# Output projections by token tile, x tiles normed one at a time, a larger ring, and loads issued by ScalarE

## The chip, the cores and the metric

One Trainium2 chip; the kernel is one launch on one NeuronCore. The metric is the device time of the launch in microseconds (us). The core's engines each run their own instruction stream in order: TensorE (PE: matmuls and transposes), VectorE (DVE), ScalarE (ACT), GpSimd (POOL) and SyncE (SP, which here only issues loads). They wait for each other, and for transfers, by semaphores.

## The reference, cut to what matters

Everything is fp32. `first_block` runs two layers on x (256 tokens of width 1024) and, in layer 0 only, on a context of 256 tokens:

```
mod = silu(c) @ w_mod[i] + b_mod[i]                  # six vectors: shifts, scales and gates
h   = modulate(rmsnorm(x) * g_pre_mix, shift, scale)
y   = concat(MLA attention, short conv, two-way SSD)(h @ w_in) @ w_out
x   = x + gate * rmsnorm(y) * g_post_mix
h   = modulate(rmsnorm(x) * g_pre_ffn, shift2, scale2)
x   = x + gate2 * rmsnorm(relu(h @ w_ff1)**2 @ w_ff2) * g_post_ffn
```

`second_block` then runs two attention mixers, a (dilated windows) and b (sliding window with sinks). After each:

```
x = layer_norm(ALPHA * x + attn(x @ w_in) @ w_out, ln_g, ln_b)
x = x + sigmoid(x @ ple_w_gate) * (p @ ple_w_proj)
```

## The kernel before

**Tiles.** Tokens come in tiles of 128: tiles 0 and 1 are the context (`CTX`), tiles 2 and 3 are x (`X`; t2 and t3 below). A residual tile is two halves of 128x512. Products with a weight block are built from 128x512 or 128x256 matmuls over 8 slices of the inner dimension (`KT`).

**fp32 from three matmuls.** Each operand is split in a high part (ACT cast, line 226) and a low part (DVE or POOL subtract, line 227); `mm3` (line 207) runs three matmuls per slice: high x high, high x low, low x high. Weights come through SP in `raw` tiles of 512 KB (`wblk`, line 170, issue at line 180; five such tiles). Their two parts go to the pools `wh` and `wl` of ten tiles each, or, for the last `keep` slices, into the `un` ring, where they may stay. Rings `qn`, `pn` and `rn` hold other working tiles.

**Norms.** `postnorm` (line 427) takes the sum of squares of a projected tile (ACT, line 431), multiplies by the gate (POOL and DVE, line 432), forms the root on POOL (lines 167 and 168) and adds to the residual (DVE, line 435). `normed` (line 400) does the same kind of chain for the next norm: ACT line 406, POOL 167 and 168, DVE 410. `modulated` (line 414) transposes a normed tile on PE (line 420), applies scale and shift while it evicts (DVE, line 424) and splits the result (lines 226, 227).

**The places of the change.** `out_projection(i)` (line 877) multiplies the mixer's output by `w_out`, column block 0 for all tiles and then column block 1, and calls `postnorm` and `done` as tiles are complete: in layer 0 for the pair X, then for the pair CTX; in layer 1 for t2 and then t3. `done` (`mid0`, line 1297; `mid1`, line 1319) is norm and modulation for the FFN, whose first block in layer 0 (lines 935 and 937) computes the columns of X, then those of CTX. `second(i)` (line 1227) is `w_out` of a mixer, the deep norm and the gate: block 0 for both tiles, block 1 for both tiles, then layer norm (DVE lines 1241 to 1250) and transposes (line 998); its rows of `ln_g` and `ln_b` are broadcast by SP (`brow`, line 235). `load_cols(1)` (line 247) loads 8 small vectors of layer 1 (line 254), transposes them (line 257) and copies them (line 259). `load_mask` (line 1028) and the rope tables (lines 1326, 1328) are small loads issued by POOL.

**What sets the order.** Each engine's order is fixed at build: a scheduler with a modelled timeline goes through the program (line 1362) and takes instructions by readiness and by the priority that decorators give some functions. Loads of all engines share a few completion semaphores; an issue that reuses one waits first until the transfer that used it before has landed.

## Time and profile before

| | |
|---|---|
| runs | 1542.83, 1542.24, 1540.04 us; median 1542.24 us |
| profiled execution | 1545.77 us; span of its trace 1544.0 us; mean granted PE clock 0.984 |
| PE busy | 1474.4 us, 95% of the span, 8417 matmuls and transposes |
| DVE, ACT, POOL busy | 67%, 48%, 20% of the span |
| DMA | 235.46 MB, 153 GB/s on average |

Busy shares are of the span. A matmul row shows a start and a modelled duration; matmuls are pipelined, so the distance from one start to the next is the pace. "idle before" is what an engine waited just before the row, and the arrow names what released it.

### The profile page before, as it was taken

What the parts mean: (1) busy time and instruction counts of PE and PEld (TensorE: products, weight loads), DVE (VectorE), ACT (ScalarE), POOL (GpSimd) and SP (SyncE); (2) the same over time, 40 slices, a digit from 0 to 9 for tenths busy, and PEclk for the clock granted to TensorE, in tenths of its full rate; (3) what the DMA queues carried; (4) which work ended last, traced back from release to release, by engine and by line L of the source; (5) the groups of instructions that cost most, each with busy time, mean ns of one, the idle gap of its engine ahead of it and who ended that gap; (6) DMA issues with size and microseconds to landing.
All of it is one profiled execution on the core that took longest, in us unless ns stands there. A gap on an engine that the chain in (4) does not pass through costs nothing.

```text
span 1544.0 us, 23412 instructions
## 1 busy us (share of the span) xinstructions
PE 1474.4 (95%) x8417; PEld 1216.4 (79%) x8417; DVE 1036.5 (67%) x2053; ACT 740.0 (48%) x1590; POOL 307.3 (20%) x356
## 2 busy tenths in 40 slices
PE   5997999999999999998999899999999999999998
PEld 3666678888878888877897688997888889878886
DVE  3559556378597557477886756676775786476866
ACT  3433335463233333245556655564566457445663
POOL 1225201151011110034330301112310320021110
PEclk9998999999999999999999999999999999999999
DMA  8844722226366546323423546555436550645442
GB/s 285 272 165 134 254 82 83 89 61 213 110 210 210 179 141 209 124 81 110 124 74 111 174 137 206 191 193 174 152 108 199 162 182 13 216 147 167 140 148 69
DMA packets 129575, 235.46 MB, mean 153 GB/s; under 512 B 11536, under 2 KB 29139, under 8 KB 129459
## 3 DMA queue, kind: packets, MB, share of 16 engines
q1 hardware_dynamic: 128576, 232.42, 47.0%
q0 software_dynamic: 704, 1.50, 0.3%
q8 instruction: 66, 1.08, 0.3%
q14 instruction: 50, 0.41, 0.1%
q10 hardware_dynamic: 179, 0.06, 0.0%
HBM read 232.82 MB, written 1.11 MB: 152 GB/s over the span
## 4 chain that ended last, share of the span: by engine, by line
PE 81%; DVE 9%; DMA 5%; issue 2%; ACT 2%; POOL 1%; SPq 0%; ACTq 0%; DVEq 0%; POOLq 0%
PE sc L212 46%; PE mm L212 19%; PE tp L459 3%; DVE wl L227 2%; PE fl L303 2%; DMA raw<-in_w_mod_dram 2%; DMA raw<-in_ple_w_gate_dram 1%; DVE u L778 1%; PE mm L635 1%; PE sc L1079 1%; PE fl L212 1%; PE sc L789 1%; PE sc L630 1%; DMA raw<-in_w_in_dram 1%; PE sc L1104 1%
## 5 line engine op out<-in xcount | busy, mean ns | idle before, releaser
L227 DVE TENSOR_TENSOR wl<-raw,wh 128x512 fp32r<-128x512 f32 (+1 forms) x602 | 418.8, 731 | 143.5 <-ACT wh L226 140.3
L226 ACT CAST wh<-raw 128x512 fp32r<-128x512 f32 (+1 forms) x602 | 357.5, 622 | 304.0 <-PE sc L212 112.2
L212 PE MATMUL sc<-wh,u 128*128 128x512 f32 (+2 forms) x1416 | 459.0, 392 | 2.3 <-DVE u L962 1.0
L212 PEld LDWEIGHTS sc<-wh,u 128*128 128x128 f32 x1416 | 265.5, 190 | 57.6 <-DVE u L962 2.2
L212 PE MATMUL sc<-wl,u 128*128 128x512 f32 (+2 forms) x708 | 274.1, 389 | 0.2
L212 PE MATMUL sc<-u,wh 128*128 128x256 f32 (+1 forms) x1072 | 264.2, 336 | 2.6 <-ACT wh L226 1.8
L212 PE MATMUL mm<-wh,u 128*128 128x512 f32 (+1 forms) x648 | 218.6, 393 | 1.6 <-ACT u L226 1.2
L212 PEld LDWEIGHTS sc<-u,wh 128*128 128x128 f32 x1072 | 183.8, 191 | 25.3 <-ACT wh L226 2.7
L212 PE MATMUL sc<-u,wl 128*128 128x256 f32 (+1 forms) x536 | 178.0, 335 | 0.0
L212 PEld LDWEIGHTS sc<-wl,u 128*128 128x128 f32 x708 | 134.4, 190 | 25.3 <-DVE wl L227 0.9
L945 POOL TENSOR_TENSOR r<-r 128x256 f32<-128x256 f32 (+1 forms) x60 | 64.1, 1069 | 421.6 <-ACT r L943 374.7
L212 PEld LDWEIGHTS mm<-wh,u 128*128 128x128 f32 x648 | 121.5, 188 | 26.8 <-ACT u L226 1.9
L212 PE MATMUL mm<-wl,u 128*128 128x512 f32 (+1 forms) x324 | 126.5, 390 | 0.0
L212 PE MATMUL mm<-u,wh 128*128 128x256 f32 (+1 forms) x512 | 116.7, 316 | 0.1
L212 PEld LDWEIGHTS sc<-u,wl 128*128 128x128 f32 x536 | 102.0, 191 | 9.6
L342 DVE SCALAR_TENSOR_TENSOR q<-raw,c_sT,q 128x512 f32<-128x512 f32 x112 | 84.9, 788 | 14.1 <-DMA raw<-in_w_mod_dram 13.5
L212 PEld LDWEIGHTS mm<-u,wh 128*128 128x128 f32 x512 | 85.7, 191 | 7.9 <-issue 1.7
L212 PE MATMUL mm<-u,wl 128*128 128x256 f32 (+1 forms) x256 | 80.4, 314 | 0.0
L946 DVE TENSOR_TENSOR u<-r,u 128x256 fp32r<-128x256 f32 (+1 forms) x60 | 33.6, 561 | 62.8 <-POOL r L945 60.4
L1012 POOL TENSOR_TENSOR r<-r,r 128x512 f32<-128x512 f32 (+1 forms) x30 | 44.7, 1494 | 152.6 <-DVE r L1010 152.5
L212 PEld LDWEIGHTS mm<-wl,u 128*128 128x128 f32 x324 | 61.2, 189 | 12.5 <-issue 0.8
L227 POOL TENSOR_TENSOR u<-r,u 128x256 fp32r<-128x256 f32 (+1 forms) x48 | 38.9, 817 | 122.8 <-ACT u L226 122.6
(318 smaller groups left out, 1992.2 us busy)
## 6 DMA issues: line engine op xcount, KB each, us to landing
raw<-in_w_ff_dram SPq DMA_DIRECT2D x128, 512.0 KB, 4.6
raw<-in_w_mod_dram SPq DMA_DIRECT2D x80, 512.0 KB, 4.7
raw<-in_a_w_in_dram SPq DMA_DIRECT2D x80, 512.0 KB, 3.7
raw<-in_w_in_dram SPq DMA_DIRECT2D x32, 512.0 KB, 4.5
raw<-in_b_w_in_dram SPq DMA_DIRECT2D x18, 512.0 KB, 4.9
raw<-in_w_mod_dram SPq DMA_DIRECT2D x32, 256.0 KB, 5.0
raw<-in_w_out_dram SPq DMA_DIRECT2D x16, 512.0 KB, 4.1
raw<-in_ple_w_gate_dram SPq DMA_DIRECT2D x16, 512.0 KB, 4.3
```

What stands on the lines that cost most here:

```text
L212: PE.matmul(ps, s, m, start=(i == 0), stop=(i == n - 1))
L226: ACT.copy(h, src)
L227: (eng or DVE).tensor_tensor(l, src, f(h), ALU.subtract)
L303: PE.matmul(ps[32 * g:32 * g + 32, :], sT[:, k + q, :], rs[g // per][:, q, w * (g % per):w * (g % per) + w], start=(k + q == 0), stop=(k + ...
L342: DVE.scalar_tensor_tensor(a, r[:, q, :], w, a, ALU.mult, ALU.add)
L459: PE.transpose(tp[:, b * P:(b + 1) * P], p[:, b * P:(b + 1) * P], ident)
L630: PE.matmul(ps[:, b * P:(b + 1) * P], qT[t][:, hs], kT[b][:, hs], start=True, stop=True, skip_group_check=True)
L635: PE.matmul(po[64 * e:64 * e + 64, hp * P:(hp + 1) * P], V[b // 2][:, 256 * (b % 2) + 64 * h:256 * (b % 2) + 64 * h + 64], pT[e][:, b * P: ...
L778: DVE.tensor_scalar(o, o, cs[:, t, c:c + 1], 0.0, ALU.subtract, ALU.min)
L945: POOL.tensor_tensor(f2[:, a:b], r[:, a:b], r[:, a:b], ALU.mult)
L946: DVE.tensor_tensor(l, f2[:, a:b], f(h), ALU.subtract)
L1012: POOL.tensor_tensor(a[:, 0:w], a[:, 0:w], b[:, 0:w], ALU.add)
```

## The change

In `out_projection(1)` both column blocks are loaded ahead, block 0 staying in the `un` ring (16 tiles), and each x tile runs block 0, block 1, postnorm, norm and modulation by itself. In `out_projection(0)` the second block's loop goes over t2, t3 and the pair CTX, so that x is normed and modulated one tile at a time (transposes and evictions 128 wide instead of 256; `mid0` places them with `o=`). `second(i)` does both blocks of one tile, its layer norm and its transposes before the next tile's; its `ln` rows move to the `qn` ring and are issued after the weight loads. The `un` ring has 48 tiles instead of 41. The small loads of `load_cols(1)`, `load_mask` and the two rope tables are issued by ACT instead of POOL, and the scratch of POOL's loads is cut to 1024 bytes.

```diff
--- before.py
+++ after.py
@@ -72,7 +72,7 @@
     PS = bass.MemoryType.PSUM
     cst, res, sm = pool("cst", 1), pool("res", 1), pool("sm", 40)
     raw, wh, wl = pool("raw", 5), pool("wh", 10), pool("wl", 10)
-    ring = {"u": pool("un", 41), "q": pool("qn", 8), "p": pool("pn", 4), "r": pool("rn", 7)}
+    ring = {"u": pool("un", 48), "q": pool("qn", 8), "p": pool("pn", 4), "r": pool("rn", 7)}
     dram = pool("dram", 1, space=bass.MemoryType.DRAM)
     pmm = pool("pmm", 2, space=PS)
     pfl = pool("pfl", 1, space=PS)
@@ -877,19 +877,32 @@
     def out_projection(i, ytok, done):
 
         gate = {r: mod_gate(i, 2, O_GQM, r) for r in ((0,) if i == 1 else (0, 1))}
+        if i == 1:
+            Ws = [wblk(A["w_out"][i], [(512 * n, 512)], keep=0 if n else KT) for n in range(2)]
+            for t in X:
+                y = []
+                for n in range(2):
+                    ps = AN()
+                    mm3(ps, list(zip(ytok(t), Ws[n])))
+                    y.append(ps)
+                    if n == 0:
+                        y[0] = U()
+                        ACT.copy(y[0], ps)
+                postnorm(t, y, gate[0])
+                done((t,))
+            return
         W = wblk(A["w_out"][i], [(0, 512)])
-        if i == 0:
-            for t in CTX:
-                xt[t] = [U(), U()]
-                load_x(t, SP)
+        for t in CTX:
+            xt[t] = [U(), U()]
+            load_x(t, SP)
         first = {}
-        for t in X + (() if i else CTX):
+        for t in X + CTX:
             ps = AN()
             mm3(ps, list(zip(ytok(t), W)))
             first[t] = U()
             ACT.copy(first[t], ps)
         W = wblk(A["w_out"][i], [(512, 512)])
-        for pair in ((X[0:1], X[1:2]) if i else (X, CTX)):
+        for pair in (X[0:1], X[1:2], CTX):
             for t in pair:
                 ps = AN()
                 mm3(ps, list(zip(ytok(t), W)))
@@ -1016,7 +1029,7 @@
         m = C([P, 5, 256], "c_mask", BF16, tag="c_tri")[:, 0:4, :].rearrange("p (s a) c -> p s (a c)", s=2)
         for s in range(2):
             r = R()
-            POOL.dma_start(r, A[n][:, s * 512:(s + 1) * 512])
+            ACT.dma_start(r, A[n][:, s * 512:(s + 1) * 512])
             POOL.tensor_copy(m[:, s, :], r)
         return m
 
@@ -1226,22 +1239,20 @@
 
     def second(i, oT, pp, fill, done):
         w_out = A["a_w_out_2" if i == 0 else "b_w_out_2"][0]
-        lg, lb = [U(), U()], [U(), U()]
+        st = [S(12), S(12)]
+        hT, transpose = xT()
+        W = [wblk(w_out, [(512 * n, 512)], keep=(0 if n else KT)) for n in range(2)]
+        lg, lb = [Q(), Q()], [Q(), Q()]
         for hf in range(2):
             brow(lg[hf], A["ln_g_2"][i, 512 * hf:512 * hf + 512])
             brow(lb[hf], A["ln_b_2"][i, 512 * hf:512 * hf + 512])
-        st = [S(12), S(12)]
-        hT, transpose = xT()
-        for n in range(2):
-            W = wblk(w_out, [(512 * n, 512)])
-            for t in range(2):
-                x = xt[2 + t]
+        for t in range(2):
+            x = xt[2 + t]
+            for n in range(2):
                 ps = AN()
-                mm3(ps, tok(oT, t, W))
+                mm3(ps, tok(oT, t, W[n]))
                 DVE.scalar_tensor_tensor(x[n], x[n], ALPHA, ps, ALU.mult, ALU.add)
                 DVE.bn_stats(st[t][:, 6 * n:6 * n + 6], x[n])
-        for t in range(2):
-            x = xt[2 + t]
             mv, rs = S(2), S(1)
             DVE.bn_aggr(mv, st[t])
             rpow(rs, mv[:, 1:2], None, LN_EPS)
@@ -1289,13 +1300,14 @@
     tri = C([P, 5 * P], "c_tri")
     SP.dma_start(tri, A["tri"])
 
-    cols[1], halves[1] = load_cols(1, POOL)
+    cols[1], halves[1] = load_cols(1, ACT)
     yT = mix(0, hT, W1, mod_units((0, 1), (0, 2)))
     h2, h2c, h2x = both()
     sc2 = mod_scale(0, 4, O_GPF)
 
     def mid0(pair):
-        modulated(normed(pair), 0 if pair == X else 1, sc2, mods[0][:, 24:32, :], h2x if pair == X else h2c)
+        x = pair != CTX
+        modulated(normed(pair), 0 if x else 1, sc2, mods[0][:, 24:32, :], h2x if x else h2c, o=P * (pair[0] - 2) if x else 0)
 
     out_projection(0, yT, mid0)
     sc1 = C([P, 8, 2], "c_scale1_1")
@@ -1323,9 +1335,9 @@
     out_projection(1, yT, mid1)
 
     rope_a = C([P, 384], "c_rope_a", tag="c_nrow").rearrange("p (t c) -> p t c", t=2)
-    POOL.dma_start(rope_a, A["rope_a"].rearrange("(t p) c -> p t c", p=P))
+    ACT.dma_start(rope_a, A["rope_a"].rearrange("(t p) c -> p t c", p=P))
     rope_b = C([P, 512], "c_rope_b", tag="c_srow")[:, 0:384].rearrange("p (t c) -> p t c", t=2)
-    POOL.dma_start(rope_b, A["rope_b"].rearrange("(t p) c -> p t c", p=P))
+    ACT.dma_start(rope_b, A["rope_b"].rearrange("(t p) c -> p t c", p=P))
     calls, first = [0], []
 
     def step(n=1):
@@ -1351,7 +1363,7 @@
 
 
 def kernel(**inputs):
-    nc = bacc.Bacc("TRN2", target_bir_lowering=False, num_devices=1)
+    nc = bacc.Bacc("TRN2", target_bir_lowering=False, num_devices=1, dynamic_dma_scratch_size=1024)
     arrays, aps = {}, {}
     data = {n: np.ascontiguousarray(inputs[n]) for n in USED}
     data.update(constants())
```

The change moves instructions at three places.

DVE at the end of `out_projection(0)`, before. Here `x_110`, `x_111` are the halves of t2, `x_112`, `x_113` those of t3, `q_` normed halves, `tp_` transposes, `r_` and `u_` results and their parts.

```order
L432 TENSOR_TENSOR r_2870<-sc_2842,q_2628 128x512
L435 SCALAR_TENSOR_TENSOR x_110<-r_2869,s_2868,x_110 128x512
L435 SCALAR_TENSOR_TENSOR x_111<-r_2870,s_2868,x_111 128x512
L432 TENSOR_TENSOR r_2909<-mm_2881,q_2628 128x512
L435 SCALAR_TENSOR_TENSOR x_112<-r_2908,s_2907,x_112 128x512
L435 SCALAR_TENSOR_TENSOR x_113<-r_2909,s_2907,x_113 128x512
L410 TENSOR_SCALAR q_2928<-x_110,s_2921 128x512
L410 TENSOR_SCALAR q_2929<-x_111,s_2921 128x512
L410 TENSOR_SCALAR q_2940<-x_112,s_2933 128x512
L410 TENSOR_SCALAR q_2941<-x_113,s_2933 128x512
```

And DVE at the same place now:

```order
L424 TENSOR_SCALAR r_2919<-tp_2917,c_scale_4623_2612,c_mod_122 128x128
L424 TENSOR_SCALAR r_2925<-tp_2923,c_scale_4623_2612,c_mod_122 128x128
L227 TENSOR_TENSOR wl_3551<-raw_3544,wh_3550 128x512
L424 TENSOR_SCALAR r_2931<-tp_2929,c_scale_4623_2612,c_mod_122 128x128
L227 TENSOR_TENSOR u_2605<-r_2919,u_2604 128x128
L424 TENSOR_SCALAR r_2937<-tp_2935,c_scale_4623_2612,c_mod_122 128x128
L432 TENSOR_TENSOR r_2969<-mm_2941,q_2628 128x512
L227 TENSOR_TENSOR u_2609<-r_2931,u_2608 128x128
L435 SCALAR_TENSOR_TENSOR x_112<-r_2968,s_2967,x_112 128x512
L435 SCALAR_TENSOR_TENSOR x_113<-r_2969,s_2967,x_113 128x512
L410 TENSOR_SCALAR q_2988<-x_112,s_2981 128x512
L410 TENSOR_SCALAR q_2989<-x_113,s_2981 128x512
```

Line 424's evictions of t2 (of `tp_2917` to `tp_2935`) now stand ahead of t3's postnorm (432, 435) and norm (410), where t2's and t3's postnorms and norms followed each other. PE there now (`q_2890` is of t2, `q_2988` of t3, the `sc_3079` row is the last matmul of CTX's block 1, the 128x256 rows are the first ones of the FFN):

```order
L212 MATMUL sc_3079<-wh_2838,u_616 128x512
L420 MATMUL tp_2917<-c_ident_104,q_2890 128x128
L420 MATMUL tp_2923<-c_ident_104,q_2890 128x128
L420 MATMUL tp_2929<-c_ident_104,q_2890 128x128
L420 MATMUL tp_2935<-c_ident_104,q_2890 128x128
L420 MATMUL tp_2992<-c_ident_104,q_2988 128x128
L420 MATMUL tp_2998<-c_ident_104,q_2988 128x128
L420 MATMUL tp_3004<-c_ident_104,q_2988 128x128
L420 MATMUL tp_3010<-c_ident_104,q_2988 128x128
L212 MATMUL mm_3296<-u_2596,wh_3250 128x256
```

The first transposes of t3 stand directly behind t2's last and ahead of the FFN, where before the transposes of both tiles alternated.

ACT at the start, before (`u_627` to `u_639` are casts of the attention's small weights, `u_669` onwards copies out of PSUM, `wh_783` the first cast of `w_in`'s next block):

```order
L226 CAST u_627<-raw_625 128x384
L226 CAST u_161<-r_549 128x256
L226 CAST u_633<-raw_631 128x384
L226 CAST u_163<-r_556 128x256
L226 CAST u_639<-raw_637 128x512
L541 COPY u_669<-mm_643 128x416
L541 COPY u_697<-sc_671 128x416
L554 ACTIVATE p_1151,s_1149<-u_669 128x256
L555 ACTIVATE p_1151,s_1149<-u_669 128x128
L226 CAST wh_783<-raw_781 128x512
```

And now:

```order
L254 DMA r_575<-in_g_post_mix_dram 8x128
L254 DMA r_575<-in_g_pre_ffn_dram 8x128
L254 DMA r_575<-in_g_post_ffn_dram 8x128
L254 DMA r_575<-in_sc_conv_w_dram 6x128
L254 DMA r_575<-in_ssd_conv_w_dram 18x128
L254 DMA r_575<-in_ssd_conv_b_dram 6x128
L226 CAST u_627<-raw_625 128x384
L226 CAST u_633<-raw_631 128x384
L226 CAST u_639<-raw_637 128x512
L259 COPY c_cols_586<-tp_584 128x110
L541 COPY u_669<-mm_643 128x416
L541 COPY u_697<-sc_671 128x416
```

The loads of line 254 stand ahead of the casts and copies, and the column copy (259) stands ahead of the copies of line 541.

ACT ahead of `second(0)`, before (`wh_13759` and `wh_13763` are the last casts of `w_out`'s block 0, `wh_13823` starts block 1, `u_13568` onwards are casts of the gated attention output):

```order
L226 CAST wh_13759<-raw_13757 128x512
L226 CAST wh_13763<-raw_13757 128x512
L226 CAST wh_13823<-raw_13821 128x512
L226 CAST wh_13827<-raw_13821 128x512
L1093 COPY q_13427<-mm_13402 128x512
L1093 COPY q_13454<-sc_13429 128x512
L1093 COPY q_13521<-sc_13496 128x512
L1093 COPY q_13548<-mm_13523 128x512
L226 CAST u_13568<-r_13567 128x256
L226 CAST u_13591<-r_13590 128x256
L226 CAST u_13614<-r_13613 128x256
```

And now (`u_13677` and `u_13700` are the last of those casts, `u_13723` to `u_13737` are casts of `ple_w_proj`, `u_13761` is the first cast of `w_out`'s block 0):

```order
L226 CAST u_13677<-r_13676 128x256
L226 CAST u_13700<-r_13699 128x256
L226 CAST u_13712<-tp_13709 128x256
L226 CAST u_13718<-tp_13715 128x256
L226 CAST u_13723<-raw_13721 128x512
L226 CAST u_13727<-raw_13721 128x512
L226 CAST u_13733<-raw_13731 128x512
L226 CAST u_13737<-raw_13731 128x512
L226 CAST u_13761<-raw_13759 128x512
```

The casts of `w_out`'s block 0 now stand behind the casts of the gated attention output and of `ple_w_proj`; before, they stood ahead of all of these.

## Rows read from the trace of the kernel before

**Rows 1.** Page: engines' busy shares, and the chain that ended last by engine

```profile
PE 1474.4 (95%) x8417; PEld 1216.4 (79%) x8417; DVE 1036.5 (67%) x2053; ACT 740.0 (48%) x1590; POOL 307.3 (20%) x356
...
PE 81%; DVE 9%; DMA 5%; issue 2%; ACT 2%; POOL 1%; SPq 0%; ACTq 0%; DVEq 0%; POOLq 0%
```

**Rows 2.** Windows, busy time of each engine; columns: length, busy us, PE clock, DMA share

```profile
324.00:334.00 10.00, 6.68 (x37) 5.21 (x36) 8.00 (x18) 4.31 (x12) 4.31 (x7) 0.83 0.00 0
856.00:880.00 24.00, 19.33 (x75) 13.50 (x74) 18.41 (x41) 13.74 (x36) 9.17 (x13) 0.86 0.45 148
1376.00:1392.00 16.00, 12.80 (x52) 9.32 (x51) 15.12 (x30) 8.87 (x20) 8.61 (x8) 0.89 0.51 165
1511.00:1520.00 9.00, 6.78 (x30) 4.30 (x29) 8.50 (x17) 5.17 (x13) 1.71 (x2) 1.00 0.20 61
```

**Rows 3.** Timeline, ACT, start; columns: start us, us, instruction, [idle before <-releaser]

```profile
55.24 0.51 ACT L226 CAST u<-raw 128x384 fp32r<-128x384 f32 x1
...
60.57 0.51 ACT L541 COPY u<-mm 128x416 f32<-128x416 f32 x1 [1.91 <-DVE c_dt L539]
...
63.01 1.14 ACT L226 CAST wh<-raw 128x512 fp32r<-128x512 f32 x2 [0.66 <-DMA raw<-in_w_in_dram]
```

**Rows 4.** Timeline, PE, same stretch

```profile
63.68 1.20 PE L212 MATMUL sc<-u,wh 128*128 128x512 f32 x4 [1.75 <-ACT wh L226]
```

**Rows 5.** Timeline, SP (its issues), same stretch

```profile
49.90 6.49 SPq L297 DMA_DIRECT2D raw<-in_w_mod_dram  x4
```

**Rows 6.** DMA issues 40 to 64 us: KB, median us to landing

```profile
raw<-in_w_mod_dram SPq DMA_DIRECT2D x4, 512.0 KB, 3.8
```

**Rows 7.** Source line 254: one issue by ACT, and us to landing of its 16

```profile
L254 ACTq DMA_DIRECT2D r<-in_ssd_conv_w_dram x1: 306/306/306, 7.6 to 7.6; - x1
...
DMA to landing us min/median/max: 2.7/4.0/5.4
```

**Rows 8.** Timeline, PE, end of out_projection(0)

```profile
310.81 0.60 PE L420 MATMUL tp<-c_ident,q 128*128 128x128 f32 x4
...
325.45 0.41 PE L420 MATMUL tp<-c_ident,q 128*128 128x128 f32 x2 [1.17 <-DVE q L410]
```

**Rows 9.** Timeline, DVE, same stretch

```profile
324.82 0.88 DVE L410 TENSOR_SCALAR q<-u,s 128x512 f32<-128x512 f32 x2 [0.45 <-POOL s L168]
```

**Rows 10.** Timeline, ACT, out_projection(1), the tile normed first

```profile
853.85 0.60 ACT L431 ACTIVATE r<-mm 128x512 f32<-128x512 f32 x1 [0.60 <-PE mm L212]
```

**Rows 11.** Timeline, DVE, out_projection(1), the tile normed first

```profile
859.03 0.88 DVE L410 TENSOR_SCALAR q<-x,s 128x512 f32<-128x512 f32 x2 [1.25 <-POOL s L168]
860.15 0.73 DVE L424 TENSOR_SCALAR r<-tp,c_scale,c_mod 128x128 f32<-128x128 f32 x2 [0.24 <-PE tp L420]
```

**Rows 12.** Timeline, PE, out_projection(1)

```profile
856.08 0.39 PE L212 MATMUL sc<-wh,u 128*128 128x512 f32 x1
859.66 0.66 PE L420 MATMUL tp<-c_ident,q 128*128 128x128 f32 x2 [3.19 <-DVE q L410]
...
870.29 3.01 PE L212 MATMUL mm<-u,u 128*128 128x512 f32 x12 [0.50 <-DVE u L227]
```

**Rows 13.** Timeline, ACT, ahead of second(0)

```profile
1356.21 2.20 ACT L226 CAST u<-raw 128x512 fp32r<-128x512 f32 x4
```

**Rows 14.** Timeline, PE, second(0)

```profile
1354.09 0.50 PE L212 MATMUL mm<-wh,u 128*128 128x512 f32 x1
...
1383.86 0.64 PE L212 MATMUL sc<-u,u 128*128 128x512 f32 x1 [0.98 <-ACT u L226]
```

**Rows 15.** Timeline, SP, second(0)

```profile
1358.62 0.46 SPq L235 DMA_DIRECT2D u<-in_ln_g_dram  x1
```

**Rows 16.** Timeline, ACT, ahead of second(1)

```profile
1491.14 0.90 ACT L226 CAST u<-r 128x256 fp32r<-128x256 f32 x2 [2.56 <-DVE r L1029]
```

**Rows 17.** Timeline, PE, second(1)

```profile
1487.95 0.50 PE L212 MATMUL sc<-wh,u 128*128 128x512 f32 x1
...
1514.06 0.44 PE L998 MATMUL tp<-c_ident,x 128*128 128x128 f32 x2 [0.99 <-DVE u L227]
```

## The prediction

> **What bounds the kernel.** I read the page first, for which engine ends the chain. PE is busy 95% of the span and makes up 81% of the chain that ended last; DVE is next with 9% [rows 1]. So PE's matmuls set the time, and a change that alters no matmul count can only move PE's pauses, and the matmuls that run at the lower granted clock behind a pause. All I have to price is which pauses go and which come. For that I read windows around the edited places, then the timelines of PE, and of the engine PE waits for, in each.
>
> The windows say where there is something to win. In 10 us early in the FFN of layer 0 PE is busy 6.68 us at a clock of 0.83; in 24 us around the norms behind `out_projection(1)` 19.33 at 0.86; in 16 us of `second(0)` 12.80 at 0.89; in 9 us of `second(1)` 6.78 [rows 2].
>
> **Part 1, the start (small loads from POOL to ACT): +3.5, between 0 and +6.** Before, ACT casts the attention's small weights from 55.24 us on and reaches the first weight cast of `w_in`'s next block at 63.01 [rows 3]; PE waits 1.75 us for that and starts at 63.68 [rows 4]. Now eight issues stand on ACT ahead of those casts and of that one. By the changed program each waits for the semaphore of an earlier load, the last for that of the fourth `w_mod` load. SP issues those four from 49.90 over 6.49 us, so the last goes out at about 56.4 [rows 5]; their median to landing is 3.8 us [rows 6], so ACT stands until about 60.2. One issue by ACT takes 0.31 us, and the fastest landing of these small loads is 2.7 us [rows 7]: 63.2. Then PE transposes the columns (0.4 us, an estimate from the 0.60 us of a row of four transposes [rows 8]), ACT copies them, and makes four copies instead of two and the same activations. Before, from the first copy at 60.57 to 63.01 passed 2.4 us, 0.7 of it a wait; three copies more at 0.5 each make 3.2 [rows 3]. So 66.8 instead of 63.01. I take +3.5. Zero holds if the semaphores are freed early and the landing lies under the casts; +6 if the landing takes its maximum of 5.4 [rows 7].
>
> The Trainium skill speaks against this term: "DMA: Bandwidth & Descriptors", section "Issuing engines are not separate DMA queues", says loads of all engines run on the same 16 DMA engines, and that another issuing engine only saves the sequencer's issue time, usually small. By that rule the term would be the eight issues alone, about 2.4 us of ACT, mostly under cover. Rows 3 to 7 do not show an issue on ACT that waits while casts stand behind it, so the trace does not decide.
>
> **Part 2, `out_projection(0)`: +7.5, between +5 and +10, the largest term.** Before, X's norms are covered by CTX's 48 matmuls: PE goes straight from these to X's last transposes at 310.81 [rows 8] and on into the FFN. What PE does wait for is CTX's chain (line 410 at 324.82 [rows 9], PE after 1.17 us at 325.45 [rows 8]), which stands on DVE behind X's modulation. In the changed order DVE takes t2's postnorm, norm and all eight evictions, and only then t3's postnorm. Four of those evictions wait for transposes that PE runs behind CTX's last matmul. So t3's chain can't start before about 311.2, and PE's next instructions are t3's transposes, ahead of the whole FFN: PE has nothing to run meanwhile. The price is a chain that the trace has, that of the first tile of layer 1: from the square at 853.85 [rows 10] by line 410 at 859.03 [rows 11] to PE's transposes at 859.66 [rows 12], 5.8 us. Ahead of it stand two pairs of evictions (0.73 us per pair [rows 11]) with ACT's casts of them behind: about 1.3 us until ACT takes t3's first square, and 0.5 for its second, since both halves' squares queue there. That is 7.6; I take +7.5. +5 if t3's squares, which need nothing of t2, slip in early; +10 if the clock falls for some 3 us behind such a pause, as in the window from 324 us. The pauses from 324 to 334 are not saved: CTX's chain now stands behind t3's modulation as it stood behind X's.
>
> **Part 3, `out_projection(1)`: +1, between -1 and +4.** Before, PE ended one tile's matmuls, ran the other's, and waited 3.19 us at 859.66 for the first one's norm [rows 12]. (A matmul's pace is 0.24 us: twelve in 3.01, less the last one's own 0.39, over eleven.) In the changed order PE still takes one tile's 48 matmuls and then the other's, but the tile normed first is the one it multiplied last, so nothing covers the chain of 5.8 us: 2.5 more than the 3.3 from 856.08 plus one pace to 859.66. The other tile's pauses, as the 0.50 at 870.29 [rows 12], go: the window's idle 4.7 us [rows 2] less those 3.2 is -1.5. I take +1: the attention's last outputs are also a little later, since weights of block 1 pass the `raw` tiles one by one.
>
> **Part 4, `second(0)`: +2.5, between -2 and +7.** Before, `w_out`'s first matmul ran at 1354.09 [rows 14], its casts long done. Now its first cast stands on ACT behind the casts of the gated outputs and of `ple_w_proj`, which ended at 1356.21 + 2.20 = 1358.41 [rows 13]. With a cast of 0.6 PE starts at about 1359: +4.9. The four `ln` rows, issued at 1358.62 and after at 0.47 us each [rows 15], now stand on SP before the last `w_out` loads: +1.9 if those are just in time. An idle PE loses the clock: +2, from the 0.63 us matmuls at 1383.86 [rows 14] against the pace of 0.24. Against this stands what per-token order saves, the second tile's 48 matmuls now covering the first tile's layer norm: 3.2 us of pauses and some 2.5 of slow matmuls in 1376 to 1392 [rows 2], about -6. Sum 4.9 + 1.9 + 2 - 6 = 2.8; I take 2.5. If nothing is saved it is +7; if the late start costs only its 4 us and more is saved, -2.
>
> **Part 5, `second(1)`: 0, between -3 and +2.** The same exchange. Before, `w_out` ran from 1487.95 [rows 17] between attention matmuls; now its first cast stands behind the last gated casts, 1491.14 + 0.90 [rows 16], so what PE did of `w_out` in the 4.4 us up to the end of that first cast, about 1492.4, moves behind it: +3.6, with under 1 us of attention between. The pauses around 1514.06 [rows 17], 2.2 us in that window [rows 2], and the waits behind it go: -3.6.
>
> **Part 6, free edits: 0.** Mask and rope loads are needed tens of us after their issue; the cover is that distance, and without it each is one landing of 4 us. The larger ring only takes away waits for a buffer, and in none of the rows above is a buffer what PE waited for.
>
> **Sum.** 3.5 + 7.5 + 1 + 2.5 + 0 = +14.5 on the profiled execution: 1545.8 + 14.5 = 1560.3. That execution is 3.5 above the median of the runs, so the forecast is 1556.8, rounded to 1557.
>
> **Rivals.**
> - *The moved loads and the later starts are covered, and only t3's chain counts.* If ACT's issues cost it only their 0.31 us each [rows 7], under the 1.9 us that it waited at 60.57 anyway [rows 3], the start is 0; with 7.5, +1, -2 and -1 the sum is 5.5: 1548. The page named in part 1 states this rule. For it: ACT is busy 48% [rows 1] and not the bound; against it: its program order.
> - *The covers work* (faster): t3's transposes follow t2's without a pause, because its postnorm runs on DVE and ACT under CTX's 48 matmuls (11.5 us at the pace, against a chain of 5.8). It decides at the moment DVE can take t3's line 432: if that is before CTX's last matmul, part 2 falls from +7.5 to -3 (CTX's chain then also starts earlier), and with parts 1, 3, 4 and 5 at 0, -1, -6 and -3.6 the time is 1542 - 13.6 = 1528.6. Against it: DVE's order, which puts t3 behind evictions that wait for PE.
> - *Every new pause also costs the clock*: 1.5 to 2 us at each of four places on top of the sum, +7: 1564.
> - That the change doesn't do what it says is possible in one sense only: the order shows the tiles separate, but in `out_projection(0)` not overlapped.
>
> **How the numbers follow.** A measurement tells about 0.2%, 3.1 us, from no change. Chances: forecast 0.58 (1552 to 1562), only t3's chain 0.18 (1545 to 1552), covers work 0.10 (1525 to 1540), clock lost as well 0.14 (1562 to 1570). The range of 1545 to 1567 leaves out the covers' case and the end of the last, together under 0.2. Faster 0.10, from the covers' case; same 0.10, from the low half of the first rival; slower 0.80.
>
> **What would show it.** In the changed trace: ACT's first weight cast of the 63 us block near 66.8; PE idle 7 to 8 us before the transposes of t3, released by DVE line 410, and the pauses behind them still there; PE idle near 5.8 before the first transposes after `out_projection(1)`; `w_out`'s first matmul of `second(0)` directly behind its cast, and no pauses before line 998 afterwards. The forecast is wrong if line 432 of t3 starts under CTX's matmuls, or if ACT's issues do not hold up the casts behind them.

## The result, and the profile after

The changed kernel takes 1584.17 us (median of 4 runs, 1582.83 to 1585.13) against 1542.53 us: ratio 1.0265, 95% interval 1.0246 to 1.0285. It is 41.6 us slower, where 14.5 were forecast. The profiled execution took 1583.46 us, span 1581.6, mean granted clock 0.976.

The page, engines' busy shares and the chain that ended last (compare [rows 1]):

```profile
PE 1483.7 (94%) x8417; PEld 1222.1 (77%) x8417; DVE 1035.8 (65%) x2065; ACT 736.3 (47%) x1598; POOL 293.7 (19%) x346
...
PE 76%; DVE 11%; DMA 6%; ACT 3%; issue 2%; POOL 1%; SPq 0%; ACTq 0%; DVEq 0%
```

PE does the same 8417 instructions. Its idle time (span less busy) grew from 69.6 to 97.9 us, by 28.3, and its busy time by 9.3 us, mostly matmuls at the lower clock: 37.6 us together. (The rest of the 41.6 is that the profiled execution of before stood 3.2 above its median, and this one stands 0.7 below.)

**Where the time went.** Both kernels have 8417 PE instructions, so I set the start of the k-th one in the one trace against the k-th in the other. The difference grows at a few places only:

| place (us in the trace after) | forecast | found |
|---|---|---|
| start, 60 to 180 | +3.5 | +4.5 |
| end of `out_projection(0)`, 315 to 345 | +7.5 | +11.4 |
| rope load in layer 1, about 794 | 0 | +2.4 |
| attention's end and `out_projection(1)`, 848 to 901 | +1 | +2.9 and +6.8 |
| `second(0)`, its start; its layer norm | +8.8; -6 (taken as +2.5) | +7.9; +2.8 |
| `second(1)` | 0 | +0.5 |
| other | 0 | -1.4 |

Windows of the changed kernel (columns as in [rows 2]):

```profile
317.00:327.00 10.00, 2.34 (x8) 1.44 (x9) 7.43 (x17) 4.41 (x15) 4.68 (x9) 0.58 0.41 136
338.00:348.00 10.00, 7.11 (x36) 5.48 (x35) 7.48 (x18) 4.26 (x13) 4.33 (x7) 0.72 0.00 1
877.00:901.00 24.00, 13.86 (x48) 9.48 (x47) 15.23 (x30) 12.72 (x33) 6.61 (x12) 0.79 0.33 108
1380.00:1393.00 13.00, 7.65 (x33) 5.44 (x30) 8.10 (x15) 8.00 (x17) 2.40 (x4) 0.74 0.61 190
1412.00:1428.00 16.00, 10.87 (x43) 8.21 (x43) 15.03 (x28) 8.27 (x19) 1.70 (x2) 0.89 0.39 123
1547.00:1556.00 9.00, 7.26 (x35) 5.28 (x33) 6.48 (x14) 4.14 (x10) 0.79 (x2) 1.00 0.20 62
```

The first row is new: 10 us in which PE works 2.34, at a clock of 0.58. The second is the CTX pair's pause, still there, and the third, fifth and sixth answer to [rows 2] one by one: 13.86 of 24 where 19.33 was, 10.87 of 16 where 12.80 was, 7.26 of 9 where 6.78 was. Only the last place is better, by the share. The fourth row is the start of `second(0)`, where PE had no pause before. (The columns are start and end of the window, its length, then busy us with the number of instructions of PE, PEld, DVE, ACT and POOL, PE's granted clock as a share of full speed, the DMA engines' share and GB/s.)

**The start.** The changed kernel's timeline of ACT, first the issues (ACTq), then what stood behind them; it answers to [rows 3]:

```profile
54.27 0.33 ACTq L254 DMA_DIRECT2D r<-in_b_mod_dram  x1
...
58.29 0.34 ACTq L254 DMA_DIRECT2D r<-in_ssd_conv_w_dram  x1
59.80 0.27 ACTq L254 DMA_DIRECT2D r<-in_ssd_conv_b_dram  x1
60.11 1.45 ACT L226 CAST u<-raw 128x384 fp32r<-128x384 f32 x3 [2.90 <-DMA r<-in_g_pre_ffn_dram]
63.10 0.25 ACT L259 COPY c_cols<-tp 128x110 f32<-128x110 f32 x1 [1.54 <-PE tp L257]
...
65.54 0.64 ACT L226 CAST wh<-raw 128x512 fp32r<-128x512 f32 x1
```

And its timeline of PE, against [rows 4]:

```profile
66.24 1.22 PE L212 MATMUL sc<-u,wh 128*128 128x512 f32 x2 [3.17 <-ACT wh L226]
```

The eight issues end at 60.07, the casts that began at 55.24 before now begin at 60.11, and the first cast of `w_in`'s next block is at 65.54 instead of 63.01. PE's first matmul there is 2.6 us later than before; with the matmuls at the lower clock behind it the delay is 3.4 us from 75 to 105 us. The last 1.1 us come between 120 and 190 us, where the delay falls to 0.4 and rises again.

**`out_projection(0)`.** The timeline of PE, against [rows 8]:

```profile
317.14 0.65 PE L420 MATMUL tp<-c_ident,q 128*128 128x128 f32 x2 [1.26 <-DVE r L424]
325.01 0.69 PE L420 MATMUL tp<-c_ident,q 128*128 128x128 f32 x2 [7.23 <-DVE q L410]
...
340.90 0.44 PE L420 MATMUL tp<-c_ident,q 128*128 128x128 f32 x2 [1.26 <-DVE q L410]
```

And that of DVE:

```profile
316.68 0.72 DVE L424 TENSOR_SCALAR r<-tp,c_scale,c_mod 128x128 f32<-128x128 f32 x2
...
319.30 0.40 DVE L424 TENSOR_SCALAR r<-tp,c_scale,c_mod 128x128 f32<-128x128 f32 x1
319.62 0.67 DVE L432 TENSOR_TENSOR r<-mm,q 128x512 f32<-128x512 f32 x1
...
324.47 0.88 DVE L410 TENSOR_SCALAR q<-x,s 128x512 f32<-128x512 f32 x2 [1.89 <-POOL s L168]
```

t3's line 432 runs at 319.62, behind the evictions of t2 (line 424 at 316.68 to 319.70), its line 410 at 324.47, and PE waits 7.23 us for it; CTX's wait (340.90; 1.17 in [rows 8]) stays. Ahead of it all, at 317.14, is a wait of 1.26 us for an eviction of t2.

**`out_projection(1)`.** The timeline of PE, against [rows 12]:

```profile
852.17 0.50 PE L212 MATMUL sc<-u,u 128*128 128x512 f32 x1 [1.95 <-ACT u L226]
...
876.97 0.39 PE L212 MATMUL sc<-wh,u 128*128 128x512 f32 x1
885.02 0.66 PE L420 MATMUL tp<-c_ident,q 128*128 128x128 f32 x2 [7.66 <-DVE q L410]
```

The timeline of DVE ahead of the transposes:

```profile
883.79 0.69 DVE L227 TENSOR_TENSOR wl<-raw,wh 128x512 fp32r<-128x512 f32 x1 [3.14 <-ACT wh L226]
884.39 0.88 DVE L410 TENSOR_SCALAR q<-x,s 128x512 f32<-128x512 f32 x2
```

And that of ACT:

```profile
877.46 0.60 ACT L431 ACTIVATE r<-sc 128x512 f32<-128x512 f32 x1 [0.56 <-PE sc L212]
...
881.22 0.19 ACT L406 ACTIVATION_READ_ACCUMULATOR r<-x 128x1 f32 x1
883.14 1.14 ACT L226 CAST wh<-raw 128x512 fp32r<-128x512 f32 x2 [1.73 <-DMA raw<-in_w_ff_dram]
```

At 852.17 PE had waited 1.95 us for a cast of `w_out`. Its last matmul starts at 876.97, the first transposes at 885.02 (859.66 in [rows 12]). From ACT's square at 877.46 (it answers to the one in [rows 10]) the chain takes 7.6 us, not 5.8: line 410 did not start when its operand was ready, 882.5 (ACT's squares were done at 881.4, and two POOL steps that follow end then), since a subtract stood ahead of it on DVE, which waited 3.14 us for a cast, which waited for a `w_ff` load.

**`second(0)`.** The timeline of PE, against [rows 14]:

```profile
1385.82 0.79 PE L212 MATMUL mm<-u,u 128*128 128x512 f32 x1 [5.06 <-ACT u L226]
...
1420.50 0.50 PE L212 MATMUL sc<-u,u 128*128 128x512 f32 x1 [3.28 <-ACT u L226]
```

And that of ACT:

```profile
1383.06 5.30 ACT L226 CAST u<-raw 128x512 fp32r<-128x512 f32 x10
...
1418.24 1.14 ACT L226 CAST wh<-raw 128x512 fp32r<-128x512 f32 x2 [5.50 <-DMA raw<-in_ple_w_gate_dram]
...
1419.82 3.22 ACT L226 CAST u<-raw 128x512 fp32r<-128x512 f32 x6
```

Between 1383.06 and 1388.36 ACT makes ten casts in a row, four of `ple_w_proj` [rows 13] and then the first of `w_out`; PE starts at 1385.82 after 5.06 us. At 1420.50 PE waits 3.28 us for a cast of the gate's weights, which stands on ACT behind one that had waited 5.50 us for its load.

**`second(1)`.** The timeline of PE, against [rows 17]:

```profile
1526.67 0.50 PE L212 MATMUL sc<-u,u 128*128 128x512 f32 x1 [1.53 <-ACT u L226]
...
1553.96 0.50 PE L212 MATMUL mm<-wh,u 128*128 128x512 f32 x1 [1.53 <-ACT u L226]
```

PE waits 1.53 us for a cast of `w_out`. At the layer norm its waits of over 0.2 us add up to 2.8 us, two of them (0.83 and 0.27) behind the end of the window shown above; before they made 2.2.

**The rope table.** The timeline of ACT near 794 us:

```profile
794.33 0.41 ACTq L1338 DMA_DIRECT2D c_rope_a<-in_rope_a_dram  x1
794.78 0.63 ACT L781 ACTIVATE u<-u 128x512 f32<-128x512 f32 x1 [1.30 <-DVE u L560]
```

And that of PE:

```profile
794.15 0.41 PE L789 MATMUL sc<-u,u 128*128 128x64 f32 x2 [1.47 <-POOL p L587]
```

ACT stands 1.3 us until DVE's line 560, the last reader of that buffer, is done, and the issue and its copies come behind. PE waits 1.47 us at the same time, but for POOL; how the one leads to the other these rows do not show. Nor do they show that the load is the reason: in e4 and in e6 to e9, where the rope loads also stand on ACT and PE has the same order there, PE loses only 0.5 to 0.9 us at this place, against 2.4 in the changed kernel. In e7 (its timeline of ACT) the wait on ACT is shorter:

```profile
792.72 0.41 ACTq L1338 DMA_DIRECT2D c_rope_a<-in_rope_a_dram  x1
793.18 0.63 ACT L781 ACTIVATE u<-u 128x512 f32<-128x512 f32 x1 [0.54 <-DVE u L560]
```

### The profile page after: what moved, and what is told of

Same layout as the page of the kernel before. It is cut to its first block, busy times and chain, and to the rows that moved or that the text cites. A ratio compares the mean times of both kernels' runs of the same rounds, so it can differ in the third digit from the quotient of the medians.

```text
span 1581.6 us, 23364 instructions
## 1 busy us (share of the span) xinstructions
PE 1483.7 (94%) x8417; PEld 1222.1 (77%) x8417; DVE 1035.8 (65%) x2065; ACT 736.3 (47%) x1598; POOL 293.7 (19%) x346
## 4 chain that ended last, share of the span: by engine, by line
PE 76%; DVE 11%; DMA 6%; ACT 3%; issue 2%; POOL 1%; SPq 0%; ACTq 0%; DVEq 0%
PE sc L212 43%; PE mm L212 19%; DVE wl L227 3%; PE tp L459 3%; PE fl L303 2%; DMA raw<-in_ple_w_gate_dram 2%; DMA raw<-in_w_mod_dram 1%; PE sc L789 1%; PE sc L1092 1%; PE fl L212 1%; DVE u L778 1%; PE mm L635 1%; DMA raw<-in_w_in_dram 1%; ACT wh L226 1%; DVE q L342 1%
## 5 line engine op out<-in xcount | busy, mean ns | idle before, releaser
L227 DVE TENSOR_TENSOR wl<-raw,wh 128x512 fp32r<-128x512 f32 (+1 forms) x578 | 404.1, 735 | 152.9 <-ACT wh L226 145.9
L226 ACT CAST wh<-raw 128x512 fp32r<-128x512 f32 (+1 forms) x578 | 341.6, 620 | 300.4 <-PE sc L212 102.9
L212 PE MATMUL sc<-wh,u 128*128 128x512 f32 (+2 forms) x1368 | 441.8, 390 | 2.1 <-ACT u L226 1.0
L212 PEld LDWEIGHTS sc<-wh,u 128*128 128x128 f32 x1368 | 257.1, 190 | 56.4 <-issue 1.8
L212 PE MATMUL sc<-wl,u 128*128 128x512 f32 (+2 forms) x684 | 265.1, 390 | 0.2
L212 PE MATMUL mm<-wh,u 128*128 128x512 f32 (+1 forms) x600 | 203.8, 394 | 2.7 <-ACT u L226 2.3
L212 PEld LDWEIGHTS sc<-wl,u 128*128 128x128 f32 x684 | 129.8, 190 | 24.2 <-DVE wl L227 0.9
L212 PEld LDWEIGHTS mm<-wh,u 128*128 128x128 f32 x600 | 112.6, 189 | 26.7 <-ACT u L226 3.2
L212 PE MATMUL mm<-wl,u 128*128 128x512 f32 (+1 forms) x300 | 117.3, 391 | 0.0
L212 PE MATMUL sc<-u,u 128*128 128x512 f32 (+2 forms) x246 | 64.6, 397 | 13.7 <-ACT u L226 10.5
```

The lines of the kernel that those rows point to most:

```text
L212: PE.matmul(ps, s, m, start=(i == 0), stop=(i == n - 1))
L226: ACT.copy(h, src)
L227: (eng or DVE).tensor_tensor(l, src, f(h), ALU.subtract)
```

## Experiments

Times are medians, each set beside runs of the kernel before on the same chip (medians 1541.4 to 1543.1). "Changed" is 1584.17, and "less" is a difference from it. The intervals are of the ratio to the kernel before. Those of e1, e5, e7 and e8 overlap the changed kernel's, but of these only e5 has runs as long as the changed kernel's shortest (1582.83). The expectations give PE's waits from one start to the next (8.05 us where the timeline's idle time is 7.66).

A median holds more than the edited place. The attention of layer 1, which e1, e4, e8 and e12 leave as it is, lost 5.1 to 6.3 us in their traces and 2.9 in the changed kernel's. So each median is read together with PE's delay over its place.

**One part undone at a time.** In each, only the lines shown go back to what they were before; `...` stands for lines left out.

e1, the small loads of the start:

```diff
-    cols[1], halves[1] = load_cols(1, ACT)
+    cols[1], halves[1] = load_cols(1, POOL)
```

> The changed kernel with only load_cols(1) issued by POOL again. Theory (four separate losses, each at its own place): the 3.4 to 4.6 us lost between 60 and 180 us go, the other three stay, so 1580 us (4 below the changed kernel), PE at w_in's next block near 63.7 us again. Rival (the loads on ACT are covered, and the early loss comes from another order of the same work): 1584, unchanged. Rival 2 (the losses hang together, an early shift sets the later ones): more than 8 us less.

1579.65 us, ratio 1.0238 (1.0215 to 1.0260): 4.5 less, and no run of it is as long as one of the changed kernel. PE reaches `w_in`'s block early again (e1's timeline of PE):

```profile
62.67 1.21 PE L212 MATMUL sc<-u,wh 128*128 128x512 f32 x4 [0.71 <-ACT wh L226]
```

e2, `out_projection(0)`:

```diff
-        for pair in (X[0:1], X[1:2], CTX):
+        for pair in (X, CTX):
```

> The changed kernel with only the second block of out_projection(0) in pairs (X, CTX) again. Theory (separate losses): PE's 7.6 us wait before t3's transposes and the half clock behind it go, about 11 us: 1573. Rival (the pause only moves to the CTX pair, whose chain then ends later): 1580 or more.

1572.73 us, 1.0196 (1.0172 to 1.0221): 11.4 less. The stretch that held the wait is full again (a window of e2):

```profile
310.00:326.00 16.00, 15.88 (x107) 14.28 (x106) 13.24 (x25) 10.11 (x24) 7.39 (x9) 1.00 0.41 132
```

e3, `out_projection(1)` by column block:

```diff
-        if i == 1:
...
-            return
...
-        for t in CTX:
...
+        if i == 0:
+            for t in CTX:
...
-        for t in X + CTX:
+        for t in X + (() if i else CTX):
...
-        for pair in (X[0:1], X[1:2], CTX):
+        for pair in ((X[0:1], X[1:2]) if i else (X[0:1], X[1:2], CTX)):
```

> The changed kernel with only out_projection(1) by column block again. Theory (separate losses): the wait of 8.05 us behind it falls to 3.6, the 2.2 us wait of the attention for w_out's casts goes, with the half clock 9 to 10 us: 1574.5. Rival (the loss there comes from the rope loads on ACT and the larger ring, not from the token order): at most 3 us less, 1581.

1575.60 us, 1.0211 (1.0185 to 1.0237): 8.6 less.

e4, `second(i)` as before the change, both mixers:

```diff
-        W = [wblk(w_out, [(512 * n, 512)], keep=(0 if n else KT)) for n in range(2)]
-        lg, lb = [Q(), Q()], [Q(), Q()]
+        lg, lb = [U(), U()], [U(), U()]
...
-        for t in range(2):
-            x = xt[2 + t]
-            for n in range(2):
+        for n in range(2):
+            W = wblk(w_out, [(512 * n, 512)])
+            for t in range(2):
```

> The changed kernel with only second(i) by column block again (both mixers). Theory (separate losses): the 5.3 us wait for w_out's first cast and the half clock behind it go (7.9), and 2 to 3 us around the layer norm: 10 us less, 1574. Rival (the wait comes from the ACT queue of the gated casts anyway, whatever the order of the products): 2 us less or nothing, 1582.

1572.55 us, 1.0192 (1.0166 to 1.0219): 11.6 less.

e5, the rope tables:

```diff
-    ACT.dma_start(rope_a, ...
+    POOL.dma_start(rope_a, ...
```

(and `rope_b` likewise)

> The changed kernel with only the two rope tables issued by POOL again. Theory (an issue on ACT that waits for its destination blocks what is queued behind it): ACT no longer stands 1.3 us near 794 us for the buffer of the first rope table, PE's 1.86 us wait there goes: 2 to 3 us less, 1581.5. Rival (free, as forecast): 1584.

1581.93 us, 1.0266 (1.0248 to 1.0283). That interval overlaps the changed kernel's, and so do the runs, so the total does not tell. Over the place PE's delay grew by 0.5 us instead of 2.4, and the wait of 1.47 us is gone; but with the loads left on ACT it grew by 0.5 to 0.6 in e6 to e9 as well. That the issuer of the rope tables costs anything is therefore not shown.

e10, all five places undone, so that of the change the ring of 48, the small scratch and the mask loads on ACT remain:

> All orders as before; of the change only the ring of 48 tiles, the small scratch and the mask loads on ACT stay. Theory (the five places are the whole loss): 1542 to 1545, no difference from before that can be told. Rival (ring or masks have a share of their own, since the five single effects of 4.5, 11.4, 8.6, 11.6 and 2.2 us add up to 38 of 42): 1546 to 1548.

1542.48 us, 1.0003 (0.9991 to 1.0015). What remains costs nothing that can be told; the five edits undone here are the whole loss, and the rope tables are part of it only by e5's unclear 2.2. The single effects add up to 38.3 of the 41.6.

**Why the wait in `out_projection(0)`.** e8 does both x tiles' postnorms first; narrow evictions and one tile at a time stay:

```diff
-        for pair in (X[0:1], X[1:2], CTX):
+        for pair in (X, CTX):
...
-            done(pair)
+            for part in ((X[0:1], X[1:2]) if pair == X else (CTX,)):
+                done(part)
```

> The changed kernel, but out_projection(0) does both x tiles' postnorms before the first tile's norm and modulation; evictions stay 128 wide and one tile at a time. Theory (the length of t3's chain that stands behind t2's evictions is the price): postnorm leaves that chain, norm stays in it, so PE's wait of 7.6 us falls to 2.5 to 4.5 us: 4 to 6 less, 1579. Rival (the price is the narrow evictions, not the chain's place): unchanged, 1584.

1579.95 us, 1.0246 (1.0231 to 1.0262): 4.2 less. The wait on PE fell from 7.23 to 2.84 us (e8's timeline of PE):

```profile
321.50 0.69 PE L420 MATMUL tp<-c_ident,q 128*128 128x128 f32 x2 [2.84 <-DVE q L410]
```

So the wait is the part of t3's chain that stands behind t2's evictions on DVE, as said. It is not the whole price: over the place e8 still loses 8.6 us where the changed kernel lost 11.4. t2's evictions still cost waits of 1.04 and 0.59 us, and in the 10 us behind the transposes (323 to 333 us) the clock is 0.75, where it was 0.91 in the changed kernel (327 to 337), so that some of the saving is lost again.

**Why the wait behind `out_projection(1)`.** e7 exchanges the blocks: block 0 goes through `wh`/`wl`, block 1 stays in the ring.

```diff
-            Ws = [wblk(A["w_out"][i], [(512 * n, 512)], keep=0 if n else KT) for n in range(2)]
+            Ws = [wblk(A["w_out"][i], [(512 * n, 512)], keep=KT if n else 0) for n in range(2)]
```

> The same exchange of blocks in out_projection(1) alone. Theory: PE has w_out matmuls for the attention's pauses again (four of 0.5 to 2.2 us between 842 and 852), 3 to 5 us less; the wait of 8 us before the first transposes stays, since PE still multiplies first the tile that is normed last: 1580. Rival (the late casts cause that wait too): 1573.

1578.22 us, 1.0237 (1.0223 to 1.0251): 6.0 less, and the long wait stays (e7's timeline of PE):

```profile
879.42 0.66 PE L420 MATMUL tp<-c_ident,q 128*128 128x128 f32 x2 [7.34 <-DVE q L410]
```

Over attention and projection the trace of e7 loses 6.9 us where the changed kernel lost 9.7; the rest of the 6.0 lies elsewhere. Here no subtract stands ahead of line 410, and from the square on the chain takes 5.7 us; but the square itself stands behind casts that waited for a `w_ff` load (e7's timeline of ACT):

```profile
872.72 1.14 ACT L226 CAST wh<-raw 128x512 fp32r<-128x512 f32 x2 [3.50 <-DMA raw<-in_w_ff_dram]
873.76 0.59 ACT L431 ACTIVATE r<-sc 128x512 f32<-128x512 f32 x1
```

e9 takes t3 first, in the projection and in the FFN's first blocks:

```diff
-            for t in X:
+            for t in X[::-1]:
...
-                for t in range(2):
+                for t in (1, 0):
```

> The changed kernel, but out_projection(1) and the FFN's first blocks behind it take t3 before t2, the order in which the attention delivers them; nothing else. Theory (the wait of 8 us stands there because the tile normed first is the one PE multiplies last): the first tile's chain is covered by the second tile's 45 matmuls, 10 us at the pace, so the wait falls under 2 us and no half clock follows: 6 to 9 us less, 1577. Rival (per-token order exposes a chain whichever tile is first): the wait moves to the second tile's transposes, 1583.

1574.46 us, 1.0218 (1.0202 to 1.0233): 9.7 less. The first transposes run among the second tile's matmuls, with no wait. The window of e9 from the first of them on:

```profile
874.00:898.00 24.00, 20.01 (x86) 13.96 (x85) 19.42 (x39) 14.94 (x37) 7.50 (x11) 1.00 0.49 162
```

Full clock, and 20.01 us of 24 against 13.86 in the changed kernel and 19.33 before [rows 2]. The attention's loss is still in it (3.4 us); over attention and projection together e9 is 0.9 us behind the kernel before.

**Why `second(0)` starts late, and why its layer norm saves nothing.** e6 exchanges the blocks of `w_out` in `second` as e7 did:

```diff
-        W = [wblk(w_out, [(512 * n, 512)], keep=(0 if n else KT)) for n in range(2)]
+        W = [wblk(w_out, [(512 * n, 512)], keep=(KT if n else 0)) for n in range(2)]
```

> The changed kernel, token order kept in second(i), but block 0 of w_out goes through the wh/wl pools and block 1 stays in the un ring (the other way round). Theory (the loss is the late casts of block 0: ring tiles come free only when the mixer ends, so these casts, and the raw tiles they hold, stand behind the gated casts): PE starts w_out about 5.1 us earlier and at full clock, and the gate's weights come earlier: 8 to 12 us less, 1574. Rival (token order itself costs it, since its tiles need both blocks): at most 2 us less, 1582.

1576.16 us, 1.0227 (1.0208 to 1.0246): 8.0 less. PE goes from the attention straight into `w_out` (e6's timeline of PE):

```profile
1385.41 0.50 PE L212 MATMUL mm<-wh,u 128*128 128x512 f32 x1
```

Its delay did not grow at all at the start (31.3 us before and after it), but by 3.3 us over the layer norm. e12 does the same for the gate's weights as well:

```diff
-        W = [wblk(A["ple_w_gate_2"][i], [(512 * n, 512)], keep=(0 if n else KT)) for n in range(2)]
+        W = [wblk(A["ple_w_gate_2"][i], [(512 * n, 512)], keep=(KT if n else 0)) for n in range(2)]
```

> As e6, and the gate's block 0 also goes through the wh/wl pools instead of the ring, so that its casts stand ahead of the casts of the second tile's transposes. Theory (token order in second saves nothing at the layer norm because PE's next work, the first tile's gate, waits for casts): PE's waits of about 2 us and the half clock behind the second tile's norm go, 3 to 4 us less than e6: 1572.5. Rival (the gate's loads arrive late whatever the pool): as e6, 1576.

1568.07 us, 1.0171 (1.0157 to 1.0185): 16.1 less than changed, 8.1 less than e6, twice what was expected. The window of e12 with the layer norm:

```profile
1400.00:1416.00 16.00, 14.41 (x66) 11.10 (x65) 15.01 (x29) 6.45 (x15) 3.40 (x4) 1.00 0.49 170
```

PE 14.41 us at full clock, against 12.80 at 0.89 before [rows 2]. Over `second(0)` this kernel gains 3.0 us on the kernel before, over `second(1)` 2.4.

**Versions against the kernel before.** e11 keeps of the change only `out_projection(1)` by token, with e7's and e9's edits, and the ring of 48 and the small scratch; everything else is as before:

> Everything as before except out_projection(1) by token with t3 first, block 0 through the wh/wl pools and block 1 in the ring of 48, and the FFN's first blocks with t3 first. Theory (token order pays where the ready tile goes first and its early block is cast early): the wait of 3.6 us and the slow matmuls and small waits behind it, 6 us in all, mostly go: 1537. Rival (nothing to win there, the wait moves on to the second tile): 1542.

1546.81 us, 1.0041 (1.0028 to 1.0054): slower, and my theory fell. PE loses 2.7 us in the attention and 1.1 in the projection. On ACT the first casts of the modulated tile stood behind a cast that waited 5.68 us for its load (e11's timeline of ACT):

```profile
862.59 1.14 ACT L226 CAST wh<-raw 128x512 fp32r<-128x512 f32 x2 [5.68 <-DMA raw<-in_w_ff_dram]
863.63 0.49 ACT L226 CAST u<-r 128x128 fp32r<-128x128 f32 x2
```

e14 tries to give that load room:

```diff
-    raw, wh, wl = pool("raw", 5), pool("wh", 10), pool("wl", 10)
-    ring = {"u": pool("un", 48), ...
+    raw, wh, wl = pool("raw", 6), pool("wh", 10), pool("wl", 10)
+    ring = {"u": pool("un", 46), ...
```

> As e11, with six raw tiles instead of five and a ring of 46. Theory (e11 lost because the two casts ahead of the modulated tile's casts on ACT waited 5.7 us for a w_ff load, and loads are late since each needs a free raw tile): those casts no longer wait, PE's wait of 2 us and the half clock behind it go: 1541.5 or less. Rival (e11's loss is the order of attention and w_out on PE): as e11, 1546.

1553.14 us, 1.0064 (1.0048 to 1.0079): slower still. In its trace PE loses 4 to 5 us each, against the kernel before, from the FFN of layer 0 to the start of layer 1, in the attention of layer 1 and in `second(0)`. It changed two things, a raw tile more and two ring tiles fewer, so it settles neither; what e11 loses is left open.

e13 keeps of the change only `second` by token, with block 0 of `w_out` and gate through `wh`/`wl` as in e12, and the ring of 48 and the small scratch:

> Everything as before except second(i) by token, with block 0 of both w_out and the gate through the wh/wl pools and block 1 in the ring of 48. Theory (token order saves the pauses around the layer norm where the casts that PE needs next stand ahead; in e12 PE left second(0) 3.3 us better than before and second(1) another 2 us): 1536 to 1538, faster than before. Rival (e12's gain came out of time lost earlier in that kernel): 1542, no change.

1538.27 us, 0.9978 (0.9961 to 0.9994) over 12 runs: faster than both kernels, by 0.2% of before, about as little as can be told. In the trace PE gains 2.4 us over `second(0)` and 2.5 over `second(1)`. The first alone would prove little: e11, whose `second` is that of the kernel before, gains 2.1 there, most of it because the clock of the same stretch is 1.00 and not 0.89 (a window of e11, against [rows 2]):

```profile
1380.00:1396.00 16.00, 13.25 (x61) 9.88 (x60) 15.22 (x29) 9.42 (x20) 8.44 (x7) 1.00 0.53 171
```

What supports e13 is its 12 runs, and in e12 and e13 PE works 14.41 and 14.00 us of such a window, more than e11's 13.25 at the same clock.

e15 is e13 with e14's edit:

> As e13, with six raw tiles and a ring of 46. Theory (late loads behind a full set of raw tiles are what holds the casts): 1 to 3 us less than e13. Rival (raw tiles are not short here): as e13.

1558.83 us, 1.0100 (1.0084 to 1.0117): 20 us worse than e13. In its trace PE loses 4 to 5 us each, against the kernel before, in `out_projection(1)`, in `second(0)` and in `second(1)`, and 3.6 from the FFN of layer 0 to the start of layer 1. Which of the two edits does it no run shows alone. Fewer ring tiles can hardly be the cause in the FFN and in `out_projection(1)`: their code is here that of the kernel before, which makes do with 41. That a sixth raw tile helps is not borne out.

## Why the prediction was wrong

The direction was right, and so were the places except the rope table's; the sum was short by 23 us, of which `out_projection(1)` makes 9, `second(0)` 8, `out_projection(0)` 4 and the place of the rope table 2. The step that failed most is the one by which a chain or a layer norm was taken to cost what an undisturbed one had cost before, or nothing where other matmuls were to cover it: the loads that casts wait for were in no term.

**Part 1, right.** +3.5 forecast, +4.5 found and e1 gives 4.5. ACT was to stand until 60.2 and did until 60.07. The first cast was to come at 66.8 and came at 65.54: PE transposed the columns about 0.4 us sooner, and from their copy to that cast passed 2.4 us, not 3.2. The lower clock behind PE's longer wait made up for it (3.4 us in all at 75 us); the last 1.1 us of the 4.5 lie where traces scatter, as said below. The rule of the Trainium skill ("DMA: Bandwidth & Descriptors", section "Issuing engines are not separate DMA queues") would have had the move cost its issue time alone; here the measurement decides against that price: the eight issues themselves are 2.4 us, and what they cost is the wait for earlier loads in ACT's order.

**Part 2, mechanism right, term too small.** The wait is 7.23 us against 7.5 forecast, released by line 410 as said, and e8 shows its cause. The clock (0.58 in that window) stood only in the upper bound, and a wait of 1.26 us ahead of t2's last transposes was left out; the upper bound of 10 was already under the 11.4 found.

**Part 3, mechanism right, term missed by 9 us.** I said that nothing covers the chain, and e9 shows it. Three things were not priced. The chain took 7.6 us and not 5.8: that of the trace before had no subtract ahead of line 410 whose cast waited for a load. The matmuls behind it ran at the lower clock (0.79 over 24 us; [rows 2] had shown 0.86 for a wait less than half as long). And "a little later" for the attention's outputs was 2.9 us: block 0's casts came so late that PE had no matmuls of `w_out` to fill the attention's pauses; e7 gives back 2.0 of it, e3 all.

**Part 4, one half right, the other failed.** The late start was 4.9 us of wait, 2 of clock and 1.9 for the `ln` rows by forecast, 8.8 in all; found were 7.9, and e6 shows that it is the casts' place on ACT. Of the 7.9, 5.3 are waits (5.06 and 0.27) and about 2.5 longer matmuls, so nothing is left for the `ln` rows, though SP issued them at 1372.86 to 1380.57 us, ahead of five of the eight `w_out` loads and not behind them all, as the program's text has it. (The 2 of clock were read from a row's duration, 0.63, set against a distance of starts, 0.24; the distance there is 0.43.) The credit of 6 us was the wrong step: I read that the second tile's matmuls cover the first tile's layer norm, and did not ask what covers the second tile's. That should have been the first tile's gate; its weights' casts stood behind others that waited for loads, and the place lost 2.8 instead. e12 shows that about half of the credit is there, 3.0 us, once those casts come early, and e13 agrees with 2.4; for single traces see the caveat at e13.

**Part 5, right by luck** (0; +0.5 found). Neither term came: the wait at the start is 1.53 us where 3.6 were forecast, and the pauses around the layer norm, which were to go, are 2.8 us against 2.2. The two misses largely cancel.

**Part 6, open for the rope table.** The cover I named was the distance to its use, but the issue had to wait for the destination's last reader with ACT's copies behind it (1.3 us here, 0.5 in e7). Whether that makes the 2.4 us lost at the place is not shown, since 1.8 of them are also missing in e6 to e9, which leave the loads on ACT. The ring and the masks were free, as e10 shows.

**The rivals.** "Every new pause also costs the clock" was nearest, with 1564. Its price for the clock, 7 us on top of the sum, was about right: PE's busy time grew by 9.3 us, and the sum had 2 of clock and a credit of 2.5. What no rival had is the greater part of the miss, waits: PE's idle time grew by 28.3 us, of which the sum holds some 15 (an estimate, 14.5 less the 2 and with the 2.5). The range ended at 1567 because the upper bounds came from rows of chains that ran without foreign waits in their queues; even all of them together, +29, are less than the 37.6 found.

## What to carry to other kernels

When work is reordered so that a chain is "covered", check in each engine's order that the chain's instructions stand ahead of what the cover produces, that the tile finished first is the one taken first, and that the work that is to cover it has its weights cast; a cast or a subtract that waits for a load blocks all that is queued behind it. A kept weight block should be the one that is used later, so that the early one goes through the pool that is free. And price the clock with each new pause: here pauses of 5 to 8 us cost about another 2 to 3 (an estimate, the place's loss less its waits).

## What was not expected of the hardware

Around these pauses the granted clock is low: 0.58 over 10 us with PE busy 2.34, 0.74 over the 13 us of `second(0)`'s start, and 128x512 matmuls then start 0.43 us apart instead of 0.23, as at the lower of the two levels (1.2 instead of 2.4 GHz). Whoever sums pauses only misses this: 9.3 of the 37.6 us are PE's longer busy time. Nor is the price fixed: with nearly the same waits, 16 us around the layer norm of `second(0)` ran at 0.89 in the kernel before and in e10 and at 1.00 in e11.

The early stage differs from execution to execution: at the 1000th PE instruction (about 185 us) the ten kernels with the changed start (the changed one, e2 to e9 and e12) were 2.6 to 9.5 us behind the trace before, with the same order of PE instructions to that point. Four with the small loads issued as before (e1, e10, e11 and e13) were 0.6 to 7.6 behind it. A place's cost is therefore read between the place's two ends, not from the start, and for the start itself e1's medians count more than one trace.
